# A squared-ReLU MLP on one core: the second product's operands, the rounding of the squares, and the order of the weight preparation

## The chip, the cores and the metric

The kernel runs as one program on 1 core of a Trainium2 chip. The metric is the device time of the program in microseconds (us). Before the change it is 3473.32 us, the median of 3 runs (3473.17 to 3486.33).

## The reference

One step of a model with two layers. A layer normalises and modulates its rows, projects them, runs three kinds of attention and a Fourier mix, projects back, and ends with an MLP. There are 1024 latent and 128 context rows of 1024 numbers. The change touches the MLP alone:

```
D_MODEL = 1024; SEQ = 128; DEC_SEQ = 1024; DEPTH = 2; D_FF = 4 * D_MODEL

def sqrelu_mlp(h, lp):
    return jnp.square(jax.nn.relu(h @ lp["mlp_w1"])) @ lp["mlp_w2"]

# in each layer, for context rows and for latent rows:
x = x + g2 * sqrelu_mlp(modulate(x, lp["norm_mlp_g"], sh2, sc2), lp)
```

Everything is float32. One matmul of the chip in a narrow type isn't exact enough, so the kernel splits each operand into a high and a low part and sums three products: high x high, high x low, low x high.

## The kernel before, in words

The activations stand transposed: 8 tiles of 128 features x 1152 rows (1024 latent, 128 context). The MLP (`mlp`) walks over 16 pairs of hidden tiles, 2 x 128 hidden units each. A pair goes through these steps:

- **First product.** For pair 0 it is a plain product (`plain`). For pairs 1 to 15 it is a seven-product scheme on 2 x 2 blocks (`seven`): the sums and differences of blocks of W1 and of the activations are multiplied, and their results combined in four PSUM banks. It is in float16 parts, after W1 has been scaled by a power of two. Matmuls have 512 columns; the context rows have a small product of their own (`context`, 128 columns).
- **Activation.** `act` takes the relu on ScalarE with the scale undone (line 1771), then the square rounded to fp32r as the high part on ScalarE (1774), the square in float32 on VectorE (1775), and their difference as the low part on VectorE (line 303, the helper `sub`).
- **Second product.** `down` takes the rows in three blocks of 384. For each of 8 output tiles it sums six matmuls of 384 columns (2 hidden tiles x 3 part products, both operands in fp32r parts) in one of six rotating PSUM banks. VectorE then multiplies the bank by the gate and adds it to the residual (`resid`, line 1684).

Weights come from HBM through the SyncE queue. `st1` and `st2` issue the loads of a pair's W1 and W2. `sp1(c + 1)` prepares W1 of the next pair: maxima on VectorE (1711), the maximum over partitions on GpSimd (1713), a scale, the scaling of both tiles (one on VectorE, 1724, one on ScalarE, 1726), and the parts of seven combinations (`put`, `h_split`, line 2008 and the helpers `acopy`, 306, and `sub`, 303). `sp2(c)` splits W2 into fp32r parts: a copy on ScalarE (306) and a subtraction on GpSimd (303).

Each engine works through its queue strictly in the order of the built program. A scheduler sets that order from the order of the code, priorities (`pri`) and the buffers that are free, so the code's order is a wish: preparation floats up into the second product of the pair before. An instruction that waits holds up all behind it on its engine.

Of the kernel before, what the change touches and what calls it, by code (L numbers as in the profile page):

```python
# [21 lines left out]
D = 1024  # L22
KT = 8
# [180 lines left out]
class Kern:  # L204
# [1475 lines left out]
    def resid(self, l, j, m, b, p, x, order=None):  # L1680
        for o, w, s in order or [(lambda t, a=c0, c=c1: t[:, a:c],) * 2 + (s,) for c0, c1, s in self.segs(b)]:
            xs = w(self.blocks(x, b)[m])
            with self.pri(RE_PRI):
                self.nc.vector.scalar_tensor_tensor(xs, o(p), self.mods[:, l, 8 * j + m, s:s + 1], xs, op0=ALU.mult,  # L1684
                                                    op1=ALU.add)

    def mlp(self, l, H, x, pre):
# [3 lines left out]
        W, W2, S1, S2, A = {}, {}, {}, {}, {}  # L1691
# [8 lines left out]

        def sp2(c):
            W2[c] = [self.split(s, [128, D]) for s in S2.pop(c)]

        def sp1(c):
# [4 lines left out]
            m = self.sm([128, 6], "wm", bufs=3)  # L1709
            for i in range(2):  # L1710
                nc.vector.reduce_max(m[:, i:i + 1], s[i].t, axis=AX.XY, apply_absolute_value=True)
            nc.vector.tensor_tensor(m[:, 2:3], m[:, 0:1], m[:, 1:2], ALU.max)  # L1712
            nc.gpsimd.partition_all_reduce(m[:, 3:4], m[:, 2:3], 128, bass_isa.ReduceOp.max)  # L1713
            sc, un = m[:, 4:5], m[:, 5:6]
            nc.vector.tensor_scalar(m[:, 3:4], m[:, 3:4], 1e-20, None, op0=ALU.max)
            nc.vector.reciprocal(sc, m[:, 3:4])
# [3 lines left out]
            nc.vector.tensor_tensor(un, un, H["un"], ALU.mult)  # L1720
            for v in s:
# [12 lines left out]
            put(11, a11)  # L1734
            put(12, a12)
            put(22, a22)
# [3 lines left out]
            put(1, s1.t)  # L1740
            if c:
# [5 lines left out]
                put(3, s1.t)  # L1747
                self.sub(nc.gpsimd, s1.t, a12, s2.t)
# [17 lines left out]
        def act(c, i, c0, src, r=None):  # L1766
# [68 lines left out]
        def down(c, b):  # L1835
            while (l, 5, 7) not in self.ready:
                yield WAIT
            d = slice(FULL[b], FULL[b] + TB)
            for m in range(KT):
# [6 lines left out]
                self.resid(l, 5, m, b, p, x, self.order(b))  # L1846
# [15 lines left out]
        for c in range(NF // 2):  # L1862
            A[c] = [[self.t([128, NT], F32R) for _ in range(2)] for _ in range(2)]
            sp2(c)
            yield from plain(c) if c == 0 else seven(c)
# [4 lines left out]
            st2(c + 1)  # L1870
            if c == 0:
                st1(1)
            prep = sp1(c + 1)
# [353 lines left out]
```

## Time and profile before

| what | value |
|---|---|
| time, median of 3 | 3473.32 us |
| the profiled execution | 3479.49 us |
| its span on the core | 3477.7 us |
| TensorE matmul busy | 3157.0 us, 91% |
| VectorE busy | 2305.5 us, 66% |
| ScalarE busy | 1449.4 us, 42% |
| GpSimd busy | 1470.8 us, 42% |

PE is TensorE, PEld its weight loads, DVE VectorE, ACT ScalarE, POOL GpSimd, SP SyncE. L281 is line 281, the helper that issues every matmul; L303 the helper for subtractions, L306 the one for copies on ScalarE. So tiles and shapes tell the uses apart: psD are the rotating banks of the MLP. A busy matmul time holds time in which matmuls overlap; how many are done in a stretch says more.

### The profile page before, as it was taken

To read this page: it belongs to the slowest core of one execution; us is meant where nothing else is said; L and a number is where in the kernel's file an instruction comes from. 1 tells how busy PE (TensorE), PEld (TensorE's weight loads), DVE (VectorE), ACT (ScalarE), POOL (GpSimd) and SP (SyncE) were. 2 spreads that over 40 slices of the span, in tenths; PEclk is the share of its full clock that TensorE was granted. 3 is DMA by queue.
4 is the path that set the end of the run, shared out by engine and by line. 5 is a ranking of instruction groups with operands and counts; after the bars stand their busy time and mean duration, and the time that the engine had idled before them with its cause. 6 is when DMAs were issued, how large, how long until landed. Compare 5 with 4: busy or idle time off the path is not lost. (4 is left out here: it accounts for less than half of the span.)

```text
span 3477.7 us, 59866 instructions
## 1 busy us (share of the span) xinstructions
PE 3157.0 (91%) x23650; PEld 2569.5 (74%) x23650; DVE 2305.5 (66%) x4887; ACT 1449.4 (42%) x2338; POOL 1470.8 (42%) x1140
## 2 busy tenths in 40 slices
PE   7997888889988999999989978799999899999998
PEld 5886666677975777777779866667788677777776
DVE  6874565645386777777687656665444877777776
ACT  4332565667263222322243326567654422222232
POOL 1331466767363322232253226678655522222332
PEclk8998798999999999999999988899999999999998
DMA  6642444334211111111036433332440111111111
GB/s 217 206 146 86 133 139 165 89 91 124 80 49 43 43 49 37 49 49 37 30 107 220 148 95 122 128 111 73 118 139 25 55 43 49 49 37 49 49 37 55
DMA packets 140547, 310.86 MB, mean 89 GB/s; under 512 B 16613, under 2 KB 85682, under 8 KB 140266
## 3 DMA queue, kind: packets, MB, share of 16 engines
q1 hardware_dynamic: 134858, 300.85, 26.4%
q10 hardware_dynamic: 5408, 6.18, 0.5%
q8 instruction: 186, 3.05, 0.4%
q14 instruction: 95, 0.78, 0.1%
HBM read 233.87 MB, written 72.82 MB: 88 GB/s over the span
## 5 line engine op out<-in xcount | busy, mean ns | idle before, releaser
L281 PE MATMUL psD<-pg,pg 128*128 128x384 f32 (+3 forms) x11129 | 2084.5, 345 | 91.2 <-DVE pg L1813 23.8
L303 POOL TENSOR_TENSOR pg<-pg,pg 128x1024 f16<-128x1024 f32 (+8 forms) x741 | 1204.7, 1640 | 1398.9 <-ACT pg L306 598.0
L281 PEld LDWEIGHTS psD<-pg,pg 128*128 128x128 f32 x8184 | 1412.9, 191 | 68.9 <-DVE pg L303 23.6
L281 PEld LDWEIGHTS <-pg 128*128 128x128 f16 x11448 | 631.2, 101 | 464.7 <-issue 111.3
L306 ACT ACTIVATE pg<-pg 128x512 f16<-128x512 f32 (+9 forms) x585 | 339.9, 613 | 735.4 <-PE psD L281 298.9
L1684 DVE SCALAR_TENSOR_TENSOR pg<-psD,mods,pg 128x256 f32<-128x256 f32 (+1 forms) x1088 | 519.3, 510 | 187.4 <-PE psD L281 187.1
L281 PE MATMUL psA<-pg,pg 128*128 128x128 f16 (+7 forms) x2746 | 508.1, 296 | 92.5 <-DVE mx L1327 31.6
L303 DVE TENSOR_TENSOR pg<-pg,pg 128x512 f16<-128x512 f32 (+12 forms) x607 | 468.4, 788 | 97.2 <-ACT pg L306 70.4
L1327 DVE TENSOR_REDUCE mx<-psA 128x1 f32<-128x384 f32 x512 | 281.5, 555 | 218.7 <-PE psA L281 205.4
L1373 ACT ACTIVATE pg<-psB 128x1024 f32<-128x1024 f32 x320 | 301.5, 945 | 256.4 <-PE psB L281 227.4
L281 PEld LDWEIGHTS psA<-pg,pg 96*128 96x128 f32 (+2 forms) x1377 | 257.4, 210 | 150.8 <-DVE mx L1327 46.7
L281 PE MATMUL psB<-pg,pg 97*128 97x512 f32 (+3 forms) x1064 | 330.2, 427 | 17.9 <-ACT pg L1373 13.1
L281 PE MATMUL psC<-pg,pg 128*128 128x65 f16 (+1 forms) x7008 | 333.2, 201 | 11.2 <-POOL pg L303 9.7
L1380 ACT ACTIVATE pg<-pg 128x1024 f16<-128x1024 f32 x320 | 308.3, 980 | 36.1 <-DMA pg<-mk 15.3
L281 PEld LDWEIGHTS psB<-pg,pg 97*128 97x128 f32 (+3 forms) x1064 | 202.7, 206 | 50.2 <-ACT pg L1373 15.4
L1332 DVE TENSOR_REDUCE mx<-psA 128x1 f32<-128x384 f32 x256 | 142.1, 555 | 100.9 <-PE psA L281 89.1
L1775 DVE TENSOR_TENSOR pg<-pg 128x512 f32<-128x512 f32 (+2 forms) x192 | 122.5, 650 | 70.8 <-ACT pg L1774 69.1
L1771 ACT ACTIVATE pg<-pg,wm 128x512 f32<-128x512 f32 x90 | 64.8, 720 | 176.1 <-DVE pg L1822 87.1
L1713 POOL PARTITION_ALL_REDUCE wm<-wm x32 | 12.1, 379 | 278.8 <-DVE wm L1712 169.7
L1726 ACT ACTIVATE pg<-pg,wm 128x1024 f32<-128x1024 f32 x32 | 36.9, 1154 | 205.7 <-DVE wm L1982 205.6
L531 ACT ACTIVATE pg<-pg 128x384 f32<-128x384 f32 x120 | 61.2, 521 | 138.3 <-DVE pg L1684 130.5
L306 ACT ACTIVATE pg<-psD 128x384 f32<-128x384 f32 (+3 forms) x104 | 54.8, 533 | 126.4 <-PE psD L281 122.8
(186 smaller groups left out, 1914.3 us busy)
## 6 DMA issues: line engine op xcount, KB each, us to landing
pg<-in_mlp_w SPq DMA_DIRECT2D x128, 512.0 KB
pg<-in_ada_p SPq DMA_DIRECT2D x96, 512.0 KB
pg<-in_w_out SPq DMA_DIRECT2D x16, 512.0 KB
pg<-y_dram SPq DMA_DIRECT2D x42, 192.0 KB
pg<-sk SPq DMA_DIRECT2D x16, 436.5 KB
sqp<-pg SPq DMA_DIRECT2D x36, 192.0 KB
mqp<-pg SPq DMA_DIRECT2D x36, 192.0 KB
pg<-sqp SPq DMA_DIRECT2D x16, 432.0 KB
```

What stands on the lines that cost most here:

```text
L281: self.nc.tensor.matmul(out, lhsT=lhsT, rhs=rhs, start=start, stop=stop, skip_group_check=skip)
L303: eng.tensor_tensor(out, a, b, ALU.subtract)
L306: self.nc.scalar.activation(out, in_, AF.Copy)
L531: self.nc.scalar.activation(q.t, x, AF.Square)
L1327: nc.vector.reduce_max(mx[:, t, i:i + 1], p[:, 0:TB], axis=AX.X)
L1332: nc.vector.reduce_max(mx[:, t, 2:3], p[:, 128:512], axis=AX.X)
L1373: nc.scalar.activation(e[:, 0:n], src, AF.Exp, scale=M["scale"])
L1380: nc.scalar.activation(pp[:, 0, 0:n], e[:, 0:n], AF.Copy)
L1684: self.nc.vector.scalar_tensor_tensor(xs, o(p), self.mods[:, l, 8 * j + m, s:s + 1], xs, op0=ALU.mult, op1=ALU.add)
L1726: nc.scalar.activation(v.t, v.t, AF.Identity, scale=sc)
L1771: nc.scalar.activation(r.t, src, AF.Relu, scale=W[c][1])
L1775: nc.vector.tensor_tensor(r.t, r.t, r.t, ALU.mult)
```

## The change

- `sp2` scales W2 by a power of two, and splits it into float16 parts instead of fp32r. The scaling is on ScalarE, two tiles of 1024 columns per pair (line 1724 of the changed kernel); copy and subtraction stay where they were.
- The scale needs the maximum of W2 of the pair. `max2` takes it on VectorE (1704). For pairs 1 to 15 it goes through the same maximum over partitions as W1's (1751, two columns now); for pair 0 it goes through TensorE (`all_max`).
- A second power of two, `rr`, is folded into the relu's scale so that the squares fit float16. Its bound comes from `h_scale`. `gates` folds the inverse of both into the gate (line 1734), and `resid` multiplies by that.
- `act` squares on ScalarE in float32 and in place, copies to float16 on ScalarE, and subtracts on VectorE. VectorE's multiplication is gone.
- `st2(c + 1)` is issued, and `sp1(c + 1)` begun, before the first product of pair c instead of after it; its steps are advanced at each step of both products.

```diff
-    def resid(self, l, j, m, b, p, x, order=None):
+    def resid(self, l, j, m, b, p, x, order=None, gate=None):
...
+                g = self.mods[:, l, 8 * j + m, s:s + 1] if gate is None else gate[:, m, s:s + 1]
...
+        def max2(c, m):
+            for i in range(2):
+                nc.vector.reduce_max(m[:, 4 + i:5 + i], S2[c][i].t, axis=AX.X, apply_absolute_value=True)
+            nc.vector.tensor_tensor(m[:, 7:8], m[:, 4:5], m[:, 5:6], ALU.max)
+
         def sp2(c):
-            W2[c] = [self.split(s, [128, D]) for s in S2.pop(c)]
+            m = M[c]
+            if c == 0:
+                max2(c, m)
+                nc.vector.tensor_scalar(m[:, 9:10], self.all_max(m[:, 7:8], 1), 1e-12, None, op0=ALU.max)
...
+            for v in S2.pop(c):
+                nc.scalar.activation(v.t, v.t, AF.Identity, scale=sc)
+                h, lo = self.t([128, D], F16), self.t([128, D], F16)
+                self.acopy(h.t, v.t)
+                self.sub(nc.gpsimd, lo.t, v.t, h.t)
+                self.free(v)
+                W2[c].append((h, lo))
+
+        def gates(c):
+            G[c] = self.sm([128, KT, 2], "gc", bufs=2)
+            nc.vector.tensor_scalar(G[c], self.mods[:, l, 40:48, :], M.pop(c)[:, 12:13], None, op0=ALU.mult)
...
+            n = 1
+            if c:
+                max2(c, m)
+                n = 2
+            nc.gpsimd.partition_all_reduce(m[:, 8:8 + n], m[:, 6:6 + n], 128, bass_isa.ReduceOp.max)
...
             put(11, a11)
+            yield
             put(12, a12)
+            yield
             put(22, a22)
             yield
...
-            nc.scalar.activation(h[:, d], r.t, AF.Square)
-            nc.vector.tensor_tensor(r.t, r.t, r.t, ALU.mult)
-            self.sub(nc.vector, lo[:, d], r.t, h.f[:, d])
+            nc.scalar.activation(r.t, r.t, AF.Square)
+            self.acopy(h[:, d], r.t)
+            self.sub(nc.vector, lo[:, d], r.t, h[:, d])
...
-            A[c] = [[self.t([128, NT], F32R) for _ in range(2)] for _ in range(2)]
+            A[c] = [[self.t([128, NT], F16) for _ in range(2)] for _ in range(2)]
             sp2(c)
-            yield from plain(c) if c == 0 else seven(c)
+            prep = iter(())
+            if c:
+                st2(c + 1)
+                prep = sp1(c + 1)
+            for _ in plain(c) if c == 0 else seven(c):
+                next(prep, None)
+                yield
...
-            st2(c + 1)
             if c == 0:
+                st2(1)
                 st1(1)
-            prep = sp1(c + 1)
+                prep = sp1(1)
             for b in range(NB):
                 next(prep, None)
...
-                yield from down(c, b)
+                for _ in down(c, b):
+                    next(prep, None)
+                    yield
```

How the order moved, at three places of VectorE's queue. In these rows a pg name with its number is one SBUF tile, psD one bank, wm the small tile of maxima and scales, gc the scaled gate, ss to ro the steps of a reciprocal root.

First place, a pair in the middle of layer one, from its last residual additions to the first combination of the seven products (u2, line 1813 before, 1861 now). Before:

```order
L1684 SCALAR_TENSOR_TENSOR pg_705_11168<-psD_16182,mods,pg_705_11168 128x256
L1684 SCALAR_TENSOR_TENSOR pg_705_11168<-psD_16182,mods,pg_705_11168 128x128
L303 TENSOR_TENSOR pg_935_16392<-pg_922_16191,pg_935_16392 128x512
L303 TENSOR_TENSOR pg_936_16397<-pg_923_16193,pg_935_16392 128x512
L2008 CAST pg_937_16465<-pg_937_16465 128x512
L1813 TENSOR_TENSOR pg_921_16045<-psD_16208,pg_758_11850 128x512
L1775 TENSOR_TENSOR pg_920_16041<-pg_920_16041 128x512
L303 TENSOR_TENSOR pg_925_16196<-pg_920_16041,pg_924_16195 128x512
L1820 TENSOR_TENSOR pg_758_11850<-psD_16208,pg_758_11850 128x512
```


After, the same place in the pair:

```order
L1685 SCALAR_TENSOR_TENSOR pg_705_11168<-psD_16305,gc_16102,pg_705_11168 128x256
L1685 SCALAR_TENSOR_TENSOR pg_705_11168<-psD_16305,gc_16102,pg_705_11168 128x128
L1734 TENSOR_SCALAR gc_16970<-mods,wm_16367 128x16
L1861 TENSOR_TENSOR pg_863_16365<-psD_16338,pg_860_16330 128x512
L303 TENSOR_TENSOR pg_762_11950<-pg_863_16365,pg_856_16175 128x512
L2072 CAST pg_863_16365<-pg_857_16314 128x512
L1868 TENSOR_TENSOR pg_860_16330<-psD_16338,pg_860_16330 128x512
L303 TENSOR_TENSOR pg_863_16365<-pg_857_16314,pg_863_16365 128x512
L1870 TENSOR_TENSOR pg_864_16431<-psD_16339,pg_860_16330 128x512
```


The two subtractions and the cast that stood between the last residual addition and the u2 addition are gone from there; the gate instruction is new, and a subtraction and a cast now come behind u2.

Second place, the end of that pair's first product and the start of its second: line 1826 before and 1874 now are the last but one combination, 1831 and 1879 the last, which frees its bank. Before:

```order
L303 TENSOR_TENSOR pg_927_16198<-pg_758_11850,pg_926_16197 128x512
L1775 TENSOR_TENSOR pg_781_12150<-pg_781_12150 128x128
L1775 TENSOR_TENSOR pg_780_12145<-pg_780_12145 128x128
L303 TENSOR_TENSOR pg_925_16196<-pg_781_12150,pg_924_16195 128x128
L303 TENSOR_TENSOR pg_927_16198<-pg_780_12145,pg_926_16197 128x128
L303 TENSOR_TENSOR pg_758_11850<-pg_936_16397,pg_938_16469 128x512
L1711 TENSOR_REDUCE wm_16801<-pg_940_16616 128x1
L1684 SCALAR_TENSOR_TENSOR pg_698_11154<-psD_16400,mods,pg_698_11154 128x384
L1831 TENSOR_TENSOR pg_921_16045<-psD_16209,pg_921_16045 128x512
L1684 SCALAR_TENSOR_TENSOR pg_699_11156<-psD_16408,mods,pg_699_11156 128x384
```


After:

```order
L1874 TENSOR_TENSOR pg_860_16330<-psD_16437,pg_860_16330 128x512
L303 TENSOR_TENSOR pg_859_16318<-pg_864_16431,pg_758_11857 128x512
L303 TENSOR_TENSOR pg_859_16318<-pg_860_16330,pg_758_11857 128x512
L303 TENSOR_TENSOR pg_860_16330<-pg_857_16314,pg_860_16330 128x512
L303 TENSOR_TENSOR pg_762_11950<-pg_863_16365,pg_856_16175 128x128
L303 TENSOR_TENSOR pg_859_16318<-pg_782_12617,pg_758_11857 128x128
L1879 TENSOR_TENSOR pg_863_16365<-psD_16339,pg_863_16365 128x512
L1685 SCALAR_TENSOR_TENSOR pg_698_11154<-psD_16538,gc_16536,pg_698_11154 128x384
L2072 CAST pg_865_16570<-pg_865_16570 128x512
L1745 TENSOR_REDUCE wm_16801<-pg_867_16749 128x1
L1685 SCALAR_TENSOR_TENSOR pg_699_11156<-psD_16546,gc_16536,pg_699_11156 128x384
```


Before the last combination there stand now a 512-wide and two 128-wide subtractions besides the two low parts, and a cast and the next maximum (1745) come after the first residual addition.

Third place, the start of layer one's MLP, where the second block of rows is normalised (lines 1943 before, 2003 now). Before:

```order
L1684 SCALAR_TENSOR_TENSOR pg_705_11168<-psD_12004,mods,pg_705_11168 128x256
L1684 SCALAR_TENSOR_TENSOR pg_705_11168<-psD_12004,mods,pg_705_11168 128x128
L548 COPY ss_12038<-psA_12034 128x3
L323 TENSOR_SCALAR rv_12040<-ss_12038 128x3
L328 RECIPROCAL ry_12042<-rs_12043 128x3
L330 TENSOR_SCALAR rv_12040<-rv_12040 128x3
L333 TENSOR_TENSOR rw_12047<-ry_12042 128x3
L335 TENSOR_TENSOR rw_12047<-rw_12047,rv_12040 128x3
L338 SCALAR_TENSOR_TENSOR ro_12050<-rw_12047,ry_12042 128x3
L1943 TENSOR_TENSOR pg_746_11807<-pg_698_11154,psA_12097 128x384
```


After, the same steps:

```order
L1704 TENSOR_REDUCE wm_12562<-pg_779_12556 128x1
L328 RECIPROCAL ry_12049<-rs_12050 128x3
L330 TENSOR_SCALAR rv_12047<-rv_12047 128x3
L917 COPY pg_759_11865<-am_12070 1x128
L333 TENSOR_TENSOR rw_12054<-ry_12049 128x3
L1705 TENSOR_TENSOR wm_12562<-wm_12562 128x1
L335 TENSOR_TENSOR rw_12054<-rw_12054,rv_12047 128x3
L1712 TENSOR_SCALAR wm_11817<-psA_12073 128x1
L338 SCALAR_TENSOR_TENSOR ro_12057<-rw_12054,ry_12049 128x3
L1745 TENSOR_REDUCE wm_12562<-pg_780_12558 128x1
L1716 RECIPROCAL wm_11817<-wm_11817 128x1
L1717 TENSOR_SCALAR wm_11817<-wm_11817 128x1
```


Maxima of the next pair's W2 (1704) and W1 (1745), and the scale of the first pair's W2 (1712 to 1720), now stand between the steps of the reciprocal root; before, they came much later or were not there.

## Rows read from the trace of the kernel before

**Rows 1.** The page: span, busy of TensorE, granted clock in 40 slices

```profile
span 3477.7 us, 59866 instructions
...
PE 3157.0 (91%) x23650; PEld 2569.5 (74%) x23650; DVE 2305.5 (66%) x4887; ACT 1449.4 (42%) x2338; POOL 1470.8 (42%) x1140
...
PEclk8998798999999999999999988899999999999998
```

**Rows 2.** Two stretches: start:end, length, busy of each engine (instructions), clock, DMA

```profile
1380.00:1428.00 48.00, 45.86 (x278) 35.72 (x277) 32.97 (x64) 11.53 (x20) 12.97 (x9) 1.00 0.13 44
1428.00:1476.00 48.00, 46.71 (x280) 36.23 (x279) 38.37 (x72) 14.99 (x24) 12.55 (x8) 1.00 0.13 45
```

**Rows 3.** VectorE's line 1813 in time: start, duration, instruction, count [idle before, releaser]

```profile
1077.07 0.68 DVE L1813 TENSOR_TENSOR pg<-psD,pg 128x512 f32<-128x512 f32 x1
...
1691.17 0.68 DVE L1813 TENSOR_TENSOR pg<-psD,pg 128x512 f32<-128x512 f32 x1
...
2760.71 0.68 DVE L1813 TENSOR_TENSOR pg<-psD,pg 128x512 f32<-128x512 f32 x1
...
3373.04 0.68 DVE L1813 TENSOR_TENSOR pg<-psD,pg 128x512 f32<-128x512 f32 x1
```

**Rows 4.** VectorE's residual additions in the second product, in time

```profile
1436.63 0.74 DVE L1684 SCALAR_TENSOR_TENSOR pg<-psD,mods,pg 128x256 f32<-128x256 f32 x2 [0.30 <-PE psD L281]
1437.67 0.74 DVE L1684 SCALAR_TENSOR_TENSOR pg<-psD,mods,pg 128x256 f32<-128x256 f32 x2 [0.30 <-PE psD L281]
```

**Rows 5.** Runs of matmuls on TensorE, in time

```profile
1405.18 5.34 PE L281 MATMUL psD<-pg,pg 128*128 128x512 f16 x24 [2.14 <-DVE pg L1813]
1410.35 2.84 PE L281 MATMUL psA<-pg,pg 128*128 128x128 f16 x48
...
1471.53 3.76 PE L281 MATMUL psD<-pg,pg 128*128 128x384 f32 x20 [0.59 <-DVE pg L303]
...
2673.47 4.06 PE L281 MATMUL psD<-pg,pg 128*128 128x384 f16 x24
2686.34 0.81 PE L281 MATMUL psD<-pg,pg 128*128 128x384 f16 x4 [0.55 <-POOL pg L303]
...
3443.10 4.41 PE L281 MATMUL psD<-pg,pg 128*128 128x384 f32 x24
```

**Rows 6.** Weight loads by form: count, busy us, mean ns, idle before

```profile
L281 PEld LDWEIGHTS psD<-pg,pg 128*128 128x128 f32 x8184 | 1412.9, 191 | 68.9 <-DVE pg L303 23.6 <-DVE pg L1684 13.8 <-POOL pg L303 9.8
...
L281 PEld LDWEIGHTS <-pg 128*128 128x128 f16 x11448 | 631.2, 101 | 464.7 <-issue 111.3 <-POOL pg L303 17.7 <-ACT pg L306 13.2
```

**Rows 7.** TensorE's waits over the run: for whom, us, times, longest

```profile
PE psD L281 <- DVE pg L1813: 23.8, 18, 3.3
```

**Rows 8.** VectorE, a cast and wide subtractions, in time

```profile
1404.10 0.43 DVE L2008 CAST pg<-pg 128x512 f16<-128x512 f32 x1 [2.60 <-POOL pg L303]
...
1440.62 0.69 DVE L303 TENSOR_TENSOR pg<-pg,pg 128x512 f16<-128x512 f32 x1
...
1442.65 4.27 DVE L303 TENSOR_TENSOR pg<-pg,pg 128x512 f16<-128x512 f32 x2 [0.69 <-ACT pg L306]
```

**Rows 9.** GpSimd beside the last of these, in time

```profile
1441.24 5.12 POOL L303 TENSOR_TENSOR pg<-pg,pg 128x1024 fp32r<-128x1024 f32 x2 [14.54 <-ACT pg L306]
```

**Rows 10.** Groups by line and form: ScalarE and VectorE in the MLP

```profile
L1684 DVE SCALAR_TENSOR_TENSOR pg<-psD,mods,pg 128x384 f32<-128x384 f32 x544 | 320.0, 609 | 97.7 <-PE psD L281 97.3
...
L306 ACT ACTIVATE pg<-pg 128x512 f16<-128x512 f32 x187 | 114.8, 625 | 282.7 <-POOL pg L303 122.6 <-POOL pg L1739 93.7 <-DVE pg L303 56.2
...
L1775 DVE TENSOR_TENSOR pg<-pg 128x512 f32<-128x512 f32 x120 | 85.7, 714 | 70.8 <-ACT pg L1774 69.1
...
L1711 DVE TENSOR_REDUCE wm<-pg 128x1 f32<-128x1024 f32 x64 | 77.3, 1208 | 20.6 <-DMA pg<-in_mlp_w 20.5
...
L1726 ACT ACTIVATE pg<-pg,wm 128x1024 f32<-128x1024 f32 x32 | 36.9, 1154 | 205.7 <-DVE wm L1982 205.6
```

**Rows 11.** TensorE at the first recursive pair of layer one, in time

```profile
1052.29 4.45 PE L281 MATMUL psD<-pg,pg 128*128 128x512 f16 x10 [4.37 <-POOL pg L303]
```

More of the change, by code (lines that the diff above doesn't have):

```diff
@@ L1683, in resid @@
             with self.pri(RE_PRI):
-                self.nc.vector.scalar_tensor_tensor(xs, o(p), self.mods[:, l, 8 * j + m, s:s + 1], xs, op0=ALU.mult,
-                                                    op1=ALU.add)
+                g = self.mods[:, l, 8 * j + m, s:s + 1] if gate is None else gate[:, m, s:s + 1]
+                self.nc.vector.scalar_tensor_tensor(xs, o(p), g, xs, op0=ALU.mult, op1=ALU.add)
     def mlp(self, l, H, x, pre):
         nc, I = self.nc, self.I
-        W, W2, S1, S2, A = {}, {}, {}, {}, {}
+        W, W2, S1, S2, A, M, G = {}, {}, {}, {}, {}, {}, {}
         def st1(c):
@@ L1720, in sp1 @@
             nc.vector.tensor_tensor(un, un, H["un"], ALU.mult)
+            nc.vector.tensor_scalar(rr, m[:, 8:9], H["bound"], 2.0 ** -20, op0=ALU.mult, op1=ALU.max)
+            nc.vector.reciprocal(rr, rr)
+            nc.vector.tensor_scalar(rr, rr, 2.0 ** 7, None, op0=ALU.mult)
+            self.two_power(rr, rr)
+            nc.vector.tensor_tensor(un, un, rr, ALU.mult)
+            yield
             for v in s:
@@ L1837, in down @@
                 yield WAIT
+            if b == 0:
+                gates(c)
             d = slice(FULL[b], FULL[b] + TB)
@@ L1845, in down @@
                     self.mm3(p[:, 0:TB], wh[:, cc], wl[:, cc], h[:, d], lo[:, d], i == 0, i == 1)
-                self.resid(l, 5, m, b, p, x, self.order(b))
+                self.resid(l, 5, m, b, p, x, self.order(b), G[c])
                 if c == NF // 2 - 1:
@@ L1877, in mlp @@
                     next(pre, None)
-                yield from down(c, b)
+                for _ in down(c, b):
+                    next(prep, None)
+                    yield
                 if c == NF // 2 - 1:
                     self.done_m = b + 1
+            for _ in prep:
+                pass
             st1(c + 2)
@@ L1934, in norm_mlp @@
                     yield WAIT
-                gain, H["un"] = self.h_scale(l)
+                gain, H["un"], H["bound"] = self.h_scale(l)
                 full = [self.t([128, NT]) for _ in range(KT)]
@@ L1992, in h_scale @@
         nc.vector.tensor_scalar(m[:, 2:3], m[:, 0:1], 32.0, m[:, 1:2], op0=ALU.mult, op1=ALU.add)
[L1993 removed]
+        p = self.all_max(m[:, 0:3], 3)
+        nc.vector.reduce_sum(m[:, 6:7], p[:, 0:2], axis=AX.X)
+        nc.vector.tensor_scalar(m[:, 6:7], m[:, 6:7], 1024.0, None, op0=ALU.mult)
+        nc.vector.tensor_scalar(m[:, 3:4], p[:, 2:3], 1e-20, None, op0=ALU.max)
         nc.vector.reciprocal(m[:, 4:5], m[:, 3:4])
```

30 lines of the change are left out of this document (20 added, 10 removed).

## The prediction

> **What bounds the kernel now.** I read the page first. TensorE is busy for 91% of a span of 3477.7 us and its granted clock is nine tenths or more of full speed in nearly every slice [rows 1]. A run of 3479.49 us holds that span, 6.2 us above the median of 3473.32 us; I sum against 3479.49 and subtract 6.2 at the end.
>
> The change lies in the MLP, so the stretches there are what counts. In two neighbouring stretches of 48 us within the first layer's MLP, TensorE is busy for 45.9 and 46.7 us at a granted clock of 1.00, the upper of its two levels (2.4 GHz); VectorE is busy 33.0 and 38.4 us, ScalarE 11.5 and 15.0, GpSimd 13.0 and 12.6 [rows 2]. TensorE is the bound, and VectorE is the only other engine near it.
>
> The period of one pair of hidden tiles comes from the same instruction in far-off pairs: line 1813 starts at 1077.07 and, thirteen pairs on, at 1691.17, which is 47.2 us a pair; in the second layer 2760.71 to 3373.04 gives 47.1 [rows 3].
>
> What fills such a pair: 84 matmuls of 512 columns, 48 of 128 and 144 of 384 (the second product). In the second product one output tile takes six matmuls. The residual additions that follow each tile start 1.04 us apart, and each waits 0.30 us for TensorE, so TensorE sets that pace [rows 4]: 1.04 / 6 = 173 ns per matmul, 24 tiles, 25.0 us. From the start of 24 float16 matmuls of 512 columns to the start of the next run 5.17 us pass, 215 ns each: 18.1 us. The run of 48 small ones adds 2.7 [rows 5]. Sum 45.8 us, so some 1.4 us of each pair is stall. A part of it has a name: after the first product TensorE waits 2.14 us for line 1813 [rows 5], 23.8 us over the run in 18 waits [rows 7]. Line 1813 stood behind a cast on VectorE that had waited 2.60 us for GpSimd [rows 8]. A second kind is the 0.59 us wait for a VectorE subtraction in the second product [rows 5].
>
> **The second product in float16.** 144 matmuls x 16 pairs x 2 layers = 4608 change from fp32r operands to float16. The trace has the new shape: in the first pair's product 24 float16 matmuls of 384 columns took 4.06 us and four took 0.81, which is (4.06 - 0.81) / 20 = 162.5 ns each; 24 of fp32r took 4.41 [rows 5]. Against 173.3 that is 10.8 ns, 49.8 us in all. By whole runs the difference is (4.41 - 4.06) / 24 = 14.6 ns, 67 us, the far end; the near end is nothing, if something other than operand type sets the 1.04 us. I take 49.8, since the 1.04 us was read where the change is. The weight loads point the same way: 191 ns for a four-byte tile, more than the spacing of its matmuls, and 101 ns for a float16 one [rows 6].
>
> **What is added elsewhere, per pair.** ScalarE: four wide copies to float16 at 0.63 us, two narrow ones and two scalings of 1024 columns at 1.15 [rows 10]: about 5.4 us on some 13. VectorE loses four wide multiplications at 0.71 and two narrow ones, gains two maxima at 1.21 [rows 10] and about fourteen 128x1 instructions, which I put at 0.15 us each: near zero net. GpSimd's two wide subtractions stay; their output halves in width. All of that fits under a TensorE pair of 44 us, so busy time itself costs nothing. The SyncE queue has the same number of loads, a stage earlier. What can cost is order.
>
> **The wait at the first sum goes.** In the changed order the u2 addition (line 1861) stands right behind the last residual additions and one tiny gate instruction, ahead of every cast that waits for GpSimd. TensorE needs it only after two further products of 2.6 us each, so this wait goes.
>
> **What is late next.** Behind the last product of a pair, VectorE now has one 512-wide and two 128-wide subtractions (each waiting for a ScalarE copy), then the addition of line 1879 that frees that product's bank, the first residual addition, a cast, a 1.2 us maximum, three more residual additions and only then the subtraction of line 303 that makes the low half needed by the second block of 384. At 0.69 us per wide instruction and 0.43 for the cast [rows 8], 0.61 per residual addition and 0.63 for the copy ahead [rows 10] this is about 7.7 us, and TensorE spends 8 x 0.975 = 7.8 us on the first block. It fits with nothing to spare.
>
> GpSimd, however, now starts the next weights' sums and subtractions at exactly that moment: its first add writes a tile which the last product has just finished reading. The trace shows the price of that neighbourhood: the same wide VectorE subtraction takes 0.69 us alone, while two of them took 4.27 us beside two GpSimd subtractions of 5.12 us [rows 8, 9], 1.4 us more each. The Trainium skill (SBUF — State Buffer, section Who interferes with whom) says that a VectorE instruction with two SBUF inputs and a GpSimd instruction that reads SBUF contend for a shared port pair, and whoever comes second blocks for the whole instruction. The trace agrees with the direction (0.69 to about 2.1 us). This rule speaks against the change.
>
> One such collision in half of the pairs, less what the start of the residual queue can absorb, is my guess: 0.9 us of stall per pair left where 1.4 was. Over 30 regular pairs this gains 15 us. Ends: no stall left (-42 us), or three collisions in every pair (third rival).
>
> **The first pair of a layer.** Its second weights need their own maximum over partitions, which goes through TensorE; it is queued behind two loads and two maxima (2.4 us) on VectorE, and what stands behind it on TensorE is the first product: +3 us per layer, from 0 to +6. On VectorE the next pair's maxima now stand ahead of the second block's normalisation, and each waits for its load. Against that, in the first layer these parts are begun before the plain product instead of in the middle of it; there TensorE waited 4.37 us for GpSimd at the first recursive pair, the longest of several such waits [rows 11]. I take -8 us for that, from -15 to +5, and nothing in the second layer, where the last of the new maxima still stands late. Together -2 us.
>
> **Sum.** 3479.5 - 49.8 - 15 - 2 = 3412.7 us for a profiled execution; minus 6.2, 3406.5 as the median.
>
> **Rivals.**
>
> First: the stalls go altogether. For it: line 1813's wait goes, and a four-bank product leaves banks to absorb a late addition. Then -49.8 - 42 - 10 = -102 us, 3371 us.
>
> Second: the change does not speed the matmuls, because the six-matmul pace of 1.04 us is set by banks or by VectorE, or the stalls eat just what the operands give. For it: VectorE's work in the second product (24 tiles of residual additions, four maxima, some twenty small instructions) comes to about 25 us by the rows' durations, beside 23.4 us of TensorE. Against: each residual addition now waits 0.30 us [rows 4], and a run of 24 of the same fp32r shape elsewhere takes longer than its float16 twin too, 4.41 beside 4.06 us [rows 5]. Time 3456 to 3490.
>
> Third, on the other side: the VectorE chain behind the last product becomes the bound of the pair. Three subtractions stretched by 1.4 us each put the low half 4.2 us late; a pair then loses 4.2 where it lost 1.4, 30 x 2.8 = 84 us, and with the 49.8 us of the operands the kernel is at 3473 + 34 = 3507 us. It decides from a stall of 1.4 + 49.8 / 30 = 3.1 us a pair. For it: the 4.27 us row and the order. Against: the low half comes a pair's worth of banks behind the residual additions, and in about half of the pairs the order has the cast, not the subtractions, ahead of line 1879.
>
> **How the numbers follow.** The forecast (operands gain, about 0.9 us of stall stays) has 0.52, the first rival 0.26, the second 0.13, the third 0.09. A measurement here can tell a change from none at about 0.5%, that is from 3456 to 3491 us. Forecast and first rival are faster; of the second nearly all lies within 0.5%; the third is slower: 0.78, 0.13, 0.09. The likeliest case alone is 3385 to 3440. The range that leaves out at most 2 in 10 runs from 3365, a little below the first rival, to 3470, where the second begins to hold.
>
> **What would show it.** Right: residual additions of the second product 0.975 us apart at a granted clock of 1.00; a pair of 44.5 to 45.5 us from line 1861 to line 1861; no TensorE wait for line 1861; remaining waits for line 303 at the second block of 384 or for line 1685 at a bank. Wrong: tiles still 1.04 us apart (second rival), VectorE without idle time in the second product and TensorE waiting over 3 us a pair on line 303, 1685 or 1879 (third), or a granted clock below 1.00 in regular pairs, which no row here speaks for.

## The result, and the profile after

The changed kernel takes 3425.4 us (median of 4 runs, 3423.14 to 3429.14); the kernel before, run beside it, 3478.84 us. The ratio is 0.9846, with a 95% interval of 0.9820 to 0.9872: 53 us less, 1.5%. Forecast were 3406.5 us in a range of 3365 to 3470.

The head of the page of the changed kernel; the line PEclk is TensorE's granted clock in 40 slices:

```profile
span 3422.5 us, 60243 instructions
PE 3102.8 (91%) x23658; PEld 2225.8 (65%) x23658; DVE 2271.7 (66%) x5215; ACT 1594.7 (47%) x2594; POOL 1453.2 (42%) x1140
PEclk8999798999989999999999988899999899999998
```

Busy shares hardly moved against [rows 1], and the mean granted clock of the span is as it was (0.945, before 0.947). The span is 55.2 us shorter. Where that came from is read pair by pair. Rows of TensorE in the second product of one pair (start, length, engine, tiles, shape, count, idle time before and its releaser):

```profile
1402.70 0.81 PE L281 MATMUL psD<-pg,pg 128*128 128x384 f16 x4
1403.97 1.30 PE L281 MATMUL psD<-pg,pg 128*128 128x384 f16 x7 [0.46 <-DVE pg L1685]
1405.62 6.66 PE L281 MATMUL psD<-pg,pg 128*128 128x384 f16 x40 [0.35 <-DVE pg L303]
```

Three more matmuls take 1.30 - 0.81 us, 163 ns each; 33 more take 6.66 - 1.30, 162.4 ns each. The fp32r ones of [rows 4] came every 173 ns. The two waits are of the kinds that were named: line 1685 at a bank, line 303 at the second block.

VectorE at the seam of the two products in the same pair:

```profile
1391.46 0.69 DVE L1874 TENSOR_TENSOR pg<-psD,pg 128x512 f32<-128x512 f32 x1 [1.06 <-PE psD L281]
...
1394.45 2.38 DVE L303 TENSOR_TENSOR pg<-pg,pg 128x512 f16<-128x512 f32 x2 [1.25 <-ACT pg L306]
...
1400.47 0.68 DVE L1879 TENSOR_TENSOR pg<-psD,pg 128x512 f32<-128x512 f32 x1
1401.07 0.68 DVE L303 TENSOR_TENSOR pg<-pg,pg 128x512 f16<-128x512 f32 x1
1401.67 0.60 DVE L1685 SCALAR_TENSOR_TENSOR pg<-psD,gc,pg 128x384 f32<-128x384 f32 x1
...
1426.51 0.69 DVE L1861 TENSOR_TENSOR pg<-psD,pg 128x512 f32<-128x512 f32 x1 [0.35 <-PE psD L281]
```

Line 1861, which TensorE waited for before [rows 5, 7], now itself waits for TensorE. From 1394.45 on VectorE has no idle time before the second product is nearly over. The waits of both kernels over some 590 us of regular pairs in layer one say the same (us in total, times, longest). Changed:

```profile
DVE pg L1685 <- PE psD L281: 3.6, 12, 0.4
PE psD L281 <- DVE pg L303: 5.6, 10, 2.1
PE psD L281 <- DVE pg L1685: 2.6, 6, 0.5
```

Before:

```profile
DVE pg L1684 <- PE psD L281: 39.5, 120, 0.4
```

The residual additions used to wait for TensorE 120 times; now VectorE is the one that is behind, and six banks absorb most of it.

For the sums, a pair is measured on TensorE, from the first 512-column matmul of one pair to that of the next, by the start of every matmul in the trace; the mean is over 13 pairs, from the second recursive pair of a layer to the fifteenth. Stall is what exceeds 144 x 162.5 ns (173.5 for fp32r) + 84 x 215.8 + 48 x 55.8, that is 44.21 us (45.79); so it holds TensorE's waits and also what a lower granted clock costs.

| us | before, layer one / two | after |
|---|---|---|
| pair | 47.43 / 46.99 | 45.07 / 44.99 |
| stall in it | 1.64 / 1.20 | 0.86 / 0.79 |

These 26 pairs are 56.6 us shorter: 41.1 by the operands (26 x 1.58), 15.5 by stalls. Operands in the other six second products give 9.5 more. That is 66.1, against 54.9 between the two profiled executions (3479.49 and 3424.58 us); 11.2 us were lost elsewhere, 9.5 of it at the starts of the two MLPs. From the first residual addition of the stage ahead to the second recursive pair, layer one took 240.3 us before and 239.5 after, layer two 224.6 and 228.5; two second products in each should have given 3.2. So layer one lost 2.4 us and layer two 7.1.

The stretch of layer two before, after, and in e3 (an experiment below that leaves layer two's code as it is): start:end, length, busy of TensorE, its weight loads, VectorE, ScalarE and GpSimd, granted clock, DMA.

```profile
2573.78:2798.34 224.56, 203.59 (x1252) 179.34 (x1250) 143.84 (x301) 91.54 (x186) 107.79 (x103) 0.98 0.16 53
2541.87:2770.38 228.51, 205.06 (x1256) 160.49 (x1255) 141.22 (x332) 101.24 (x203) 113.67 (x104) 0.94 0.18 59
2543.40:2767.90 224.50, 201.23 (x1256) 157.71 (x1256) 145.71 (x333) 101.57 (x203) 109.54 (x104) 0.97 0.18 61
```

TensorE's waits there are 20.6 us before and 23.4 after. The larger part of layer two's loss goes with the granted clock of the stretch, 0.94 beside 0.98: e3, at 0.97, takes 4 us less with the same code there. No experiment set the clock.

In layer one TensorE's waits grew more, from 28.2 to 37.9 us. The stretch is no longer for it, since both executions spend 27.3 us of it at the lower clock, but matmuls fill 21.3 us of that before and 12.8 after; the rest lies in waits. The largest single wait is in layer one; the same broadcast in both layers of the changed kernel:

```profile
993.40 1.62 PE L281 MATMUL psA<-ident,ro 128*128 128x128 f32 x6 [10.05 <-DVE wm L1721]
...
2664.95 0.91 PE L281 MATMUL psA<-ident,ro 128*128 128x128 f32 x6 [0.24 <-DVE ro L338]
```

The releaser named in the first row is merely VectorE's last instruction before it; the row scale itself (line 338, 993.09 to 993.25 us) ended next to it. Its lateness can be read on ScalarE: the two scalings and two copies of the first pair's W2 (lines 1724 and 306, 976.30 to 980.37 us) stand ahead of the second block's modulation (line 2005). That starts 5.1 us after the broadcast of its own row scale (975.62 us), where it started 1.5 us after it before (979.46), and the third block's row scale comes behind it.

The plain product, which could have filled the wait, was late by itself, and that is read on GpSimd. The maximum over partitions of the next pair now stands ahead of the second block's subtractions. After, and then before:

```profile
979.51 4.22 POOL L303 TENSOR_TENSOR pg<-pg,pg 128x1024 f16<-128x1024 f32 x2 [5.92 <-ACT pg L306]
989.84 0.37 POOL L1751 PARTITION_ALL_REDUCE wm<-wm  x1 [6.11 <-DVE pg L303]
996.90 6.38 POOL L303 TENSOR_TENSOR pg<-pg,pg 128x384 f16<-128x384 f32 x7 [6.69 <-ACT pg L2005]
```

```profile
982.33 0.92 POOL L303 TENSOR_TENSOR pg<-pg,pg 128x384 f16<-128x384 f32 x1 [3.44 <-ACT pg L306]
```

The subtractions of this block begin at 996.90 us now and began at 982.33 before. The inputs of the maximum were there at 981.66 us (the end of line 1746), and still GpSimd does nothing for 6.11 us ahead of it and for 6.69 behind it. All 32 such maxima of the changed kernel look like this: the instructions on either side are at least 13 us apart, for a maximum of 0.37 us. In e5 two of them follow each other, with no idle time between them:

```profile
2772.64 0.72 POOL L1719 PARTITION_ALL_REDUCE wm<-wm  x2 [6.64 <-issue]
2780.69 1.26 POOL L1745 TENSOR_TENSOR pg<-pg 128x512 f32<-128x512 f32 x1 [7.33 <-DVE pg L1828]
```

So the idle time seems to belong to the change between GpSimd's ordinary instructions and this one. The kernel before has 32 such maxima too; the change moved one of them to this place.

### The profile page after: what moved, and what is told of

The parts are those of the page before. It is cut to its first block, busy times and chain, and to the rows that moved or that the text cites. A ratio compares the mean times of both kernels' runs of the same rounds, so it can differ in the third digit from the quotient of the medians.

```text
span 3422.5 us, 60243 instructions
## 1 busy us (share of the span) xinstructions
PE 3102.8 (91%) x23658; PEld 2225.8 (65%) x23658; DVE 2271.7 (66%) x5215; ACT 1594.7 (47%) x2594; POOL 1453.2 (42%) x1140
## 4 chain that ended last, share of the span: by engine, by line
PE 58%; DVE 17%; DMA 8%; POOL 6%; issue 5%; ACT 5%; SPq 0%; ACTq 0%; DVEq 0%; POOLq 0%
PE psD L281 38%; PE psA L281 9%; PE psB L281 6%; DVE pg L303 5%; POOL pg L303 5%; PE psC L281 4%; DMA pg<-in_ada_p 3%; DVE pg L1685 2%; DMA pg<-mqr 2%; ACT pg L306 2%; DVE mx L1327 1%; DMA pg<-in_dft_lat 1%; ACT pg L1819 1%; DVE wm L1745 1%; ACT pg L1822 1%
## 5 line engine op out<-in xcount | busy, mean ns | idle before, releaser
L281 PE MATMUL psD<-pg,pg 128*128 128x384 f16 (+6 forms) x10510 | 2029.7, 341 | 76.2 <-DVE pg L303 25.4
L303 POOL TENSOR_TENSOR pg<-pg,pg 128x1024 f16<-128x1024 f32 (+8 forms) x743 | 1190.3, 1616 | 1124.9 <-ACT pg L306 413.4
L281 PEld LDWEIGHTS <-pg 128*128 128x128 f16 x16056 | 1084.9, 100 | 771.8 <-issue 120.5
L303 DVE TENSOR_TENSOR pg<-pg,pg 128x512 f16<-128x512 f32 (+11 forms) x617 | 477.8, 795 | 265.0 <-ACT pg L306 249.8
L281 PEld LDWEIGHTS psD<-pg,pg 128*128 128x128 f32 x3576 | 613.2, 194 | 39.9 <-DVE pg L303 16.1
L306 ACT ACTIVATE pg<-pg 128x512 f16<-128x512 f32 (+8 forms) x777 | 431.2, 588 | 345.8 <-POOL pg L303 78.3
L1685 DVE SCALAR_TENSOR_TENSOR pg<-psD,gc,pg 128x384 f32<-128x384 f32 (+2 forms) x1024 | 473.4, 505 | 13.5 <-PE psD L281 13.3
L281 PE MATMUL psD<-pg 128*128 128x384 f16 (+1 forms) x674 | 219.7, 328 | 8.3 <-DVE pg L303 4.8
L1785 POOL TENSOR_TENSOR pg<-pg 128x512 f32<-128x512 f32 x32 | 43.4, 1356 | 233.4 <-PE psA L281 181.6
```

The source lines that it names most:

```text
L281: self.nc.tensor.matmul(out, lhsT=lhsT, rhs=rhs, start=start, stop=stop, skip_group_check=skip)
L303: eng.tensor_tensor(out, a, b, ALU.subtract)
L306: self.nc.scalar.activation(out, in_, AF.Copy)
L1685: self.nc.vector.scalar_tensor_tensor(xs, o(p), g, xs, op0=ALU.mult, op1=ALU.add)
L1785: nc.gpsimd.tensor_tensor(s1.t, a21, a22, ALU.add)
```

## Experiments

Times are medians, ratios against the kernel before in the same set (its medians 3479 to 3486 us). "Line waits" is how long VectorE waited over the whole run for weight loads and for GpSimd's maximum over partitions before a pair's maxima or scale.

| kernel | operands | squares | scale, maxima | preparation | us | ratio, 95% | pair, layer one / two | stall | line waits |
|---|---|---|---|---|---|---|---|---|---|
| before | fp32r | VectorE | no | late | 3480 | 1 | 47.43 / 46.99 | 1.64 / 1.20 | 28 |
| e12 | fp32r | ScalarE | no | late | 3472.9 | 0.9961 (0.9945 to 0.9978) | 47.22 / 46.74 | 1.43 / 0.95 | 35 |
| e7 | fp32r | VectorE | no | early | 3483.5 | 1.0000 (0.9987 to 1.0012) | 47.58 / 46.57 | 1.79 / 0.78 | 70 |
| e1 | fp32r | ScalarE | yes | early | 3586.9 | 1.0310 (1.0287 to 1.0333) | 51.27 / 50.89 | 5.48 / 5.10 | 247 |
| e5 | f16 | VectorE | no | late | 3481.9 | 0.9998 (0.9986 to 1.0011) | 48.56 / 46.54 | 4.35 / 2.34 | 101 |
| e6 | f16 | VectorE | no | early | 3480.4 | 0.9993 (0.9981 to 1.0006) | 48.21 / 46.38 | 4.01 / 2.17 | 101 |
| e10 | f16 | ScalarE | no | early | 3456.2 | 0.9939 (0.9919 to 0.9960) | 47.30 / 45.72 | 3.09 / 1.52 | 109 |
| e9 | f16 | VectorE | yes | early | 3483.9 | 1.0009 (0.9997 to 1.0021) | 47.04 / 47.37 | 2.83 / 3.16 | 19 |
| e2 | f16 | ScalarE | yes | late | 3473.9 | 0.9981 (0.9968 to 0.9995) | 46.17 / 47.98 | 1.97 / 3.77 | 40 |
| after | f16 | ScalarE | yes | early | 3425.4 | 0.9846 (0.9820 to 0.9872) | 45.07 / 44.99 | 0.86 / 0.79 | 30 |

In every float16 build the wide matmuls of the second product come 162.5 ns apart, in every fp32r build 173.5. The other columns decide whether that is kept.

**e1, fp32r operands in the changed kernel.**

```diff
-                h, lo = self.t([128, D], F16), self.t([128, D], F16)
...
+                W2[c].append(self.split(v, [128, D]))
...
-            A[c] = [[self.t([128, NT], F16) for _ in range(2)] for _ in range(2)]
+            A[c] = [[self.t([128, NT], F32R) for _ in range(2)] for _ in range(2)]
```

> The changed kernel with the second product's operands back in fp32r parts; scaling, squares and the early preparation stay. Theory (operands): nearly all of the 53 us is the spacing of the 4608 wide matmuls, 162.5 against 173.5 ns, 50.7 us; the stalls of a regular pair stay near 1.1 us. In this build the third block's row scale stands behind most of the plain product again, so layer one's wait of 10.05 us before that scale goes too, some 8 us back. Time 3425 + 51 - 8 = 3468 us (3460 to 3478). Rival (order): the gain is the removed wait and the earlier preparation, and this stays below 3440 us.

It took 3587 us, over 100 us more than either theory allowed. 26 regular pairs are 157 us longer than in the changed kernel, 41 of it spacing and 116 stall. TensorE's waits in them are 89 us (15 in the changed kernel), 73 of it at the fourth and fifth matmul of the second product. The granted clock there is 0.97, beside 1.00 in the changed kernel, which makes up a part of the rest. VectorE in one first product of layer two:

```profile
3413.05 2.48 DVE L1704 TENSOR_REDUCE wm<-pg 128x1 f32<-128x1024 f32 x2 [4.12 <-DMA pg<-in_mlp_w]
3415.45 0.68 DVE L1857 TENSOR_TENSOR pg<-psD,pg 128x512 f32<-128x512 f32 x1
...
3419.44 0.15 DVE L1749 TENSOR_SCALAR wm<-wm 128x1 f32<-128x1 f32 x1 [3.25 <-POOL wm L1747]
```

and its waits of these two kinds over the run:

```profile
DVE wm L1749 <- POOL wm L1747: 152.4, 30, 6.9
DVE wm L1704 <- DMA pg<-in_mlp_w: 80.1, 34, 4.1
```

The maxima of the next pair, which belong into the second product, come so late that VectorE waits for them in the first, and the squares stand behind.

**e2, late preparation in the changed kernel.**

```diff
...
-                st2(c + 1)
-                prep = sp1(c + 1)
-            for _ in plain(c) if c == 0 else seven(c):
-                next(prep, None)
-                yield
+            yield from plain(c) if c == 0 else seven(c)
...
+            st2(c + 1)
+            prep = sp1(c + 1)
```

> The changed kernel with the preparation of the next pair (loads of W2, maxima, parts of W1) issued after the first product again and advanced once a block, as before the change; float16 parts, scaling and squares stay. Theory: the earlier preparation is worth only the change in stalls per pair, 1.36 to 1.1 us, some 8 us over 30 pairs: 3433 us (3426 to 3441), with a TensorE wait at the first combination (line 1861) back, about 1 us a pair. Rival one (the order carries the gain): over 3450 us. Rival two (the early preparation costs, since its GpSimd work lies beside VectorE's subtractions): under 3420 us.

3474 us: the first rival. Nearly the whole gain goes. In layer two W2, which has to pass load, maximum, scale and copy in one line, isn't there in time:

```profile
3181.76 5.34 PE L281 MATMUL psD<-pg,pg 128*128 128x512 f16 x24 [1.72 <-DVE pg L1856]
...
3200.53 0.48 PE L281 MATMUL psD<-pg,pg 128*128 128x384 f16 x1 [6.39 <-ACT pg L306]
```

The second row is the second product standing for a high half that ScalarE hasn't copied; the first is the old wait for the first combination, back again.

**e3, the row scale of layer one held back.**

```diff
...
+        while H and H.get('pl', 0) < 3:
+            yield WAIT
         pb = self.ps("A")
...
+        if H:
+            self.pin(first, [mybir.EngineType.PE])
...
```

> The changed kernel, but in layer one the broadcast of the third block's row scale is held on TensorE behind the first three quarters of the plain product, where it stood before the change (51 matmuls behind the second block's, instead of 28). Nothing else is changed on purpose. Theory: the 10.05 us wait of layer one was TensorE standing in line behind that broadcast while the plain product's matmuls were ready; most of it goes, 3425 - 8 = 3417 us (3413 to 3421), with no TensorE wait over 4 us before that broadcast. Rival: the operands of the plain product were late anyway, the wait only changes its name: 3423 to 3428 us.

3428.6 us, ratio 0.9856 (0.9833 to 0.9879): no gain, as the rival has it. TensorE in layer one:

```profile
994.42 2.08 PE L281 MATMUL psD<-pg,pg 128*128 128x384 f16 x6 [14.74 <-POOL pg L303]
```

The broadcast no longer stops the plain product, and the plain product's own operands are late, behind GpSimd's subtractions. The first of these starts at 993.47 us, 7.28 us behind the same maximum over partitions (985.82 us). No run moves that maximum by itself, so its price is read from the trace and not tested.

**e4, the low half last.** Only TensorE's order changes.

```diff
-                for i in range(2):
+                for j, i in enumerate((0, 1) if b == 0 else (1, 0)):
...
+                    self.mm(o, wh[:, cc], h[:, d], j == 0, False)
+                    self.mm(o, wl[:, cc], h[:, d], False, False)
+                    self.mm(o, wh[:, cc], lo[:, d], False, j == 1)
```

> The changed kernel with another order of the six matmuls of each output tile of the second product: weights high x squares high, weights low x squares high, and only then weights high x squares low; in the second and third block of 384 the second hidden tile goes first. VectorE and GpSimd keep their order. Theory: the stalls left at the start of the first and of the second block (4th and 49th matmul of the product, 0.35 to 0.7 us each, in about two pairs of three) are waits for the low half from the last subtractions of VectorE; needing it two to five matmuls (0.3 to 0.8 us) later removes most: 3425 - 8 = 3417 us (3413 to 3421). Rival (banks, or VectorE's pace): the stall moves on to a bank and the time stays 3423 to 3428 us.

3421.0 us, 0.9833 (0.9811 to 0.9855): not told apart from the changed kernel. Its TensorE waits over the regular pairs of layer two:

```profile
PE psD L281 <- DVE pg L1685: 2.9, 8, 0.5
PE psD L281 <- DVE pg L303: 2.1, 1, 2.1
```

In the changed kernel line 303 held TensorE nine times there and line 1685 three times (5.2 and 1.0 us). The stall moves to a bank, as the rival has it: a low half and a residual addition stand in the same queue, and VectorE's pace is the limit behind both.

**e5, e6 and e7: float16 alone, float16 with the early order, the early order alone**, all made from the kernel before, W2 unscaled.

```diff
-            W2[c] = [self.split(s, [128, D]) for s in S2.pop(c)]
...
+                h, lo = self.t([128, D], F16), self.t([128, D], F16)
+                self.acopy(h.t, v.t)
+                self.sub(nc.gpsimd, lo.t, v.t, h.t)
...
```

> The kernel before with one edit: the second product's four operands (both halves of the squares, both halves of W2) are float16 instead of fp32r. No scale and no maximum of W2, squares on VectorE as before, preparation late as before. The late order with scale and maxima measured 3474 us. Theory (late order costs through the maxima: load, maximum, scale, copy stand in one line ahead of TensorE): without them the spacing counts in full, 3480 - 51 = 3429 us (3421 to 3437). Rival (late preparation itself eats the gain, whatever is prepared): 3460 to 3478 us.

> The same float16 operands without scale and maxima of W2 and with squares as before, but with the early preparation of the change. Theory: the early order is needed only to hide the maxima; here it is worth the stalls alone, some 8 us beside the late one: 3421 us (3411 to 3429). Rival one: scale, maxima and the copies on ScalarE cost time even in the changed kernel, and without them it is under 3408 us. Rival two: GpSimd's early work beside VectorE costs, over 3432 us.

> The kernel before with the early preparation alone; fp32r operands, no scale, no maxima, squares as before. The build with fp32r, scale and early order measured 3587 us, 51 us a pair, and there ScalarE's copies waited 237 us in one layer for TensorE to leave their tile. Theory (room): fp32r halves take twice the SBUF, the early preparation gets no free tiles and its copies wait for TensorE: 3540 to 3600 us. Rival (scale and maxima made that build slow, not the tiles): 3465 to 3485 us.

All three take the time of the kernel before; each interval holds 1. The theories behind e5 and e6 fall, and room as the whole reason for e1 falls with e7. The time of e6 lies with its second rival, but no run singles out that rival's reason. In e5 and e6 TensorE's matmuls are 1.58 us a pair faster and its stalls grow by 1.0 to 2.7 us. VectorE's waits in e5 have the mark of e1:

```profile
DVE wm L1721 <- POOL wm L1719: 50.4, 24, 4.5
DVE wm L1717 <- DMA pg<-in_mlp_w: 50.4, 23, 4.4
```

Two of the built orders suggested a reason for the first line: GpSimd's maximum over partitions standing right behind two wide subtractions of W2, whose copy waits until TensorE leaves a tile. e9 and e10 were made to test that.

**e8, less room.**

```diff
+            if c == 1:
+                hold = [self.t([128, NT]) for _ in range(6)]
+                for v in hold:
+                    nc.gpsimd.memset(v[:, 0:1], 0.0)
...
```

> The changed kernel with six of its 44 SBUF pages (4.6 KB of each partition) held by unused tiles from the second to the fifteenth pair of a layer; the added instructions are six memsets of one column. Theory (room): the changed kernel lives from the pages that float16 halves free; with six fewer the copies wait for tiles TensorE still reads, pairs of 46.5 to 51 us, 3470 to 3600 us. Rival (the fp32r type itself made the other build slow): 3423 to 3432 us.

3491.9 us, 1.0025 (1.0015 to 1.0036), pairs of 47.70 and 47.45 us: the room theory, for this kernel. With six pages fewer the same waits appear:

```profile
DVE wm L1753 <- POOL wm L1751: 93.3, 28, 5.7
DVE wm L1704 <- DMA pg<-in_mlp_w: 71.4, 39, 4.7
```

The changed kernel has 12.7 and 3.8 us in these two lines. So six pages of the room, and with them the time at which copies and loads can start, are worth some 62 us here.

**e9, squares back on VectorE in the changed kernel.**

```diff
-            nc.scalar.activation(r.t, r.t, AF.Square)
-            self.acopy(h[:, d], r.t)
+            nc.scalar.activation(h[:, d], r.t, AF.Square)
+            nc.vector.tensor_tensor(r.t, r.t, r.t, ALU.mult)
```

> The changed kernel with the squares as before: ScalarE writes the high half straight from its square, VectorE multiplies in float32 (four wide multiplications of 0.69 us and two narrow ones a pair come back to VectorE, as many ScalarE copies of 0.63 us go). Scale, maxima and early preparation stay, so GpSimd's maximum over partitions stays ahead of W2's wide subtractions. Theory (order by dependence): the gain hangs on that order, which the scale forces, not on VectorE's relief: 3432 us (3422 to 3442). Rival (squares): VectorE's chain behind the last product decides, and 3.3 us more a pair on it bring back the time of the kernels without the edit: 3465 to 3490 us.

3483.9 us: the rival. The order as the whole cause falls, since this build has only 19 us of line waits. It falls by the orders themselves too: counted over all pairs, the changed kernel has the maximum right behind W2's wide subtractions in most pairs of layer two, and 12.7 us of waits for it. VectorE at the seam:

```profile
1408.91 0.69 DVE L1874 TENSOR_TENSOR pg<-psD,pg 128x512 f32<-128x512 f32 x1 [0.99 <-PE psD L281]
...
1411.06 1.55 DVE L1823 TENSOR_TENSOR pg<-pg 128x512 f32<-128x512 f32 x1
...
1416.10 1.35 DVE L1823 TENSOR_TENSOR pg<-pg 128x128 f32<-128x128 f32 x1
...
1419.03 0.68 DVE L1879 TENSOR_TENSOR pg<-psD,pg 128x512 f32<-128x512 f32 x1
```

and TensorE just behind it:

```profile
1419.77 3.44 PE L281 MATMUL psD<-pg,pg 128*128 128x384 f16 x19 [0.75 <-DVE pg L1879]
```

From line 1874, which waits for TensorE in both, to line 1879 it is 10.12 us; in the changed kernel 1400.47 - 1391.46 = 9.01. Line 1879 frees a bank, and TensorE now comes round to that bank, five tiles on, before it is free. Over the regular pairs of layer one TensorE waits 9.3 us for line 1879 and 12.8 for line 303.

**e10, squares on ScalarE in e6** (the edit of e9 the other way round).

> The kernel with float16 operands and early preparation but without scale and maxima of W2 (measured 3480 us), with one edit: squares and copies on ScalarE as in the change. Without the scale nothing ties W2's copies to the maxima; GpSimd's maximum over partitions still stands behind W2's wide subtractions. Theory (order by dependence): VectorE still waits some 40 us a layer for that maximum and some 20 to 35 us for the weight loads, 3465 to 3485 us. Rival (squares): VectorE's relief is what counts, 3420 to 3435 us.

3456.2 us, 0.9939 (0.9919 to 0.9960): between the two. By the ratios of e6 and e10 (0.9993 - 0.9939, of 3480) the squares give 19 us here although the line waits stay (109 us); by those of e9 and the changed kernel (1.0009 - 0.9846) they give 57 where these waits are gone. This build is also the changed kernel without the scale and the maxima of W2. So with the squares on ScalarE these are worth some 32 us (0.9939 - 0.9846), and with the squares on VectorE nothing (e6 and e9, 0.9993 and 1.0009). They add work, so what they bring is presumably the order that goes with them; the line waits go from 109 to 30 us.

**e12, squares on ScalarE in the kernel before** (the same edit).

> The kernel before (fp32r operands, late preparation, no scale) with one edit: the square in float32 and the copy to the high half both on ScalarE, VectorE's multiplication gone, as in the change. Theory (seam and spacing together): VectorE's line at the seam between the products costs little while TensorE's tiles take 1.04 us, since the 1.1 to 1.9 us of stall a pair is mostly not there; at most a third of it goes: 3471 us (3463 to 3480). Rival (the relief of VectorE is the whole gain, whatever the operands): 3425 to 3440 us.

3472.9 us, 0.9961 (0.9945 to 0.9978): some 14 us, as the theory has it. The relief is not the gain by itself.

**e11, a faster version.** The order of e4, and two constants that move the W1 scaling and the casts from VectorE to ScalarE.

```diff
-W_SC = (0,)
-W_HI = (0,)
+W_SC = ()
+W_HI = ()
...
```

> A try at a faster version: the changed kernel with the matmul order of the low-half-last run, and with VectorE relieved in the second product: the W1 scaling of 0.73 us and the casts of 0.42 us go to ScalarE, which waits 12 to 18 us a pair. Theory (the stalls left, 0.8 us a pair, are VectorE's pace against six banks): half of them go, 3413 us (3406 to 3420). Rival (ScalarE's longer line ahead of the copies delays W1's parts by as much): 3420 to 3435 us.

3406.7 us (3404.71 to 3415.13), ratio 0.9796 (0.9772 to 0.9820): 2.0% under the kernel before, about 0.5% under the changed one, whose interval it just touches. The only wait listed for TensorE over 13 pairs of layer one:

```profile
PE psD L281 <- DVE pg L303: 1.9, 1, 1.9
```

The pair is 44.48 us there, 0.28 of it stall; in layer two 44.90 and 0.69. The two edits were not timed apart; e4, the order alone, is not clear of the changed kernel.

## Why the prediction was right, and where it was not

**The spacing** (49.8 us) was right in size: 173.5 - 162.5 = 11.0 ns, times 4608 is 50.7 us.

**The stalls of a pair** were right too: read as 1.4 us, measured 1.64 and 1.20 in the kernel before; 0.9 left forecast, 0.86 and 0.79 measured; 15 us forecast, 15.5 over 26 pairs. The wait for line 1861 went, and line 303 at the second block and line 1685 at a bank came. The count behind the 0.9, one collision with GpSimd in half of the pairs, was too low: between lines 1874 and 1879 a 512-wide subtraction is stretched beyond 0.9 us in 22 of the 30 regular pairs, 41 in all. That the size came out all the same is in part luck. Of the two subtractions at 1394.45 the first took 1.78 us and the second 0.68, which is what one takes alone, while a GpSimd row reads

```profile
1394.45 1.78 DVE L303 TENSOR_TENSOR pg<-pg,pg 128x512 f16<-128x512 f32 x1 [1.25 <-ACT pg L306]
1394.41 1.27 POOL L303 TENSOR_TENSOR pg<-pg,pg 128x512 f32<-128x512 f32 x1
```

The subtraction ends 0.55 us after the GpSimd row. Over the regular pairs of the changed kernel 64 such 512-wide subtractions start while GpSimd is in a TENSOR_TENSOR, and every one ends 0.55 us (within 0.03) after that instruction does.

The Trainium skill (SBUF — State Buffer, section Who interferes with whom) has a VectorE instruction with two SBUF inputs contend with a GpSimd instruction that reads SBUF, and the one that comes second blocked for the whole of the other. The trace agrees, with these 64 ends.

**The first pairs and transitions** (-2 us) are the term that failed: 11.2 us were lost there and elsewhere, 9.5 of it at the starts of the two layers. The spacing and the stalls gave 1.3 us more than forecast, so the execution came to 3424.58 us where 3412.7 were summed. The step named for a loss, a wait at W2's maximum through TensorE, did not occur; no TensorE wait stands there. The -8 us for layer one, parts begun before the plain product, left out what else the change puts there: W2's scalings and copies on ScalarE, and the next pair's maximum on GpSimd, around which GpSimd does no other work for 13.2 us. TensorE's waits in that stretch grew by 9.7 us; e3 shows that the row scale, where TensorE stands for 10.05 us, is only the place where the lateness is met. In layer two, put at nothing beyond the +3 us for the maximum, waits grew by 2.8 us, and the rest goes with a granted clock of 0.94, which the prediction had no term for.

**The median.** Another 7 us of the distance from 3406.5 to 3425.4 us come from the 6.2 us that were subtracted at the end, as if the profiled execution before had been a long one. With a fourth run beside it the kernel before has a median of 3478.84 us, so the profiled execution was an ordinary one.

**"Residual additions 0.975 us apart"** could not be seen as put: VectorE no longer waits for TensorE there, so its additions follow its own queue. The spacing of the matmuls themselves answers the question.

**The terms don't stand alone**, and the prediction added them as if they did. It put the maxima, scalings and squares at "busy time itself costs nothing". e5 to e7 and e9 show what holds that up: float16 without relief of VectorE at the seam gains nothing, because the second rival's mechanism, stalls that eat what the operands give, is what a build gets by default. By ratios, the squares on ScalarE are worth 14 us with fp32r, 19 with float16 and late maxima, and 57 in the full change (e9); the scale and the maxima 32 (e10), the early preparation 47 (e2), six pages of room 62 (e8). The prediction's remark that the line behind the last product fits "with nothing to spare" (7.7 us beside 7.8) was a point on which the gain hung: e9 adds multiplications to that line, and the gain is gone.

Left open: why e1 is so much worse than e7 and before. Its waits are of the kind seen in e8, and fp32r parts take twice the room, but e7 with fp32r and the early order doesn't have them to that extent; only e1 has also the scale, which ties W2's copies to the maxima. No run separates these. Nor is it settled why the maxima are late in e5, e6 and e10, which have more room than the kernel before; that a maximum takes GpSimd 13 us of a pair of some 45 makes whatever stands before and behind it on that engine dear, but no run varies that.

## What to carry to other kernels

When the engine that bounds a kernel gets faster operands, look for the queue that hands it the next operands and frees its banks, and sum that queue over the seam alone, not over the pair: eleven nanoseconds a matmul were taken in every float16 build and kept only where VectorE's line behind the last product was short enough. Undoing one edit of a change at a time shows what each rests on; here each, taken out alone, cost from 32 us to more than the whole gain of 53. A change of tile sizes also decides when copies and loads may start: read the waits of the helper engines, not only those of the bound one. And read the idle time on both sides of an instruction that is unlike its neighbours, not only its own length.

## What was not expected of the hardware

Two things. An operation of 0.37 us, the maximum over partitions on GpSimd, goes with at least 13 us between the instructions on either side of it, in all 32 places of the changed kernel. Where VectorE waited for it, it waited 70.7 us in 26 waits in e10, beside 12.7 us in 12 in the changed kernel. And a 512-wide subtraction on VectorE that starts beside one on GpSimd isn't slowed by a share: it ends 0.55 us after the other, 64 times of 64.

The spacing of the wide matmuls was the same in all builds with one operand type, and TensorE's granted clock over the regular pairs was 0.97 to 1.00 in all of them.
